# Byte addresses of matmul operands, and attention scores on 128 rows instead of 64, in a two-block fp32 network

## The chip, the cores and the metric

One Trainium2 chip, one of its cores. The metric is the device time of one execution in microseconds, from three runs; one further execution was profiled.

## The reference, cut to what matters

Two transformer blocks over 512 tokens of width 1024, all in float32. The tokens lie along the free axis, the width along partitions (eight tiles of 128).

```
first_block:  16 meta tokens in front, so 528 columns
  h = h + 0.5*swiglu(rmsnorm(h))                       # d_ff 2816
  q,k,v,u,g_attn,g_ssm = rmsnorm(h) @ w_in
  attn = sliding_window_attention(q,k,v)               # 16 query heads, 4 key heads, head size 64
  ssm  = s5 state space model of u, then a gated linear unit
  h = h + (sigmoid(g_attn)*attn + sigmoid(g_ssm)*ssm) @ w_out
  h = h + 0.5*swiglu(rmsnorm(h))                       # meta tokens no longer needed: 512 columns
second_block: 2 layers of  mixer (MLA, then GLA), layer_norm, conv_ffn (d_ff 2816), layer_norm, gated embedding
```

In the attention, a query block of 128 tokens meets the 16 meta keys and the keys of its own and the preceding block: 272 columns, 144 for the first block. A score has a contraction of 64, the head size.

## The kernel before, in words

**How a product is made.** Every large product is done in three passes with operands split in two parts (type fp32r): weights into `whi` and `wlo`, activations into `zh` and `zl` (or `mh`/`ml`, `yh`/`yl`, `gh`/`gl`, `oqh`/`oql`, `ovh`/`ovl`, `pth`/`ptl`). `mm3` (L166) runs for each of the k tiles: `whi` x high part, `whi` x low part, `wlo` x high part, all accumulated in one PSUM bank. The weights are stationary (128 columns), the activations move: 512 columns, or 264 twice in the parts of block 1 that carry the meta tokens (`C528`, tile `mm`). `nat` (L181) has the roles exchanged: the activations are stationary and 256 columns of weights move. Scores, the transposes and a few others are plain f32 matmuls, which the trace shows as two instructions ("passes") each.

**Order.** The program is unrolled. A planner that simulates the program orders the instructions and places the waits; `hold` and `behind` fix the order at a few places. Weights are fetched from HBM with SP's queue into `raw`, split on ScalarE (L84, `whi`) and VectorE (L64, `wlo`), five deep.

**Where the operands lie.** Tiles are placed one after another in a partition, each rounded up to 32 bytes, pools on top of one another in the order in which they are opened. Only the remainder of a start address by 512 matters below, so it is given in brackets. At address 0 lies a scratch of 16384 bytes, then 128 bytes of constants, then pool `cp` (vec 1888 bytes, eight tiles h of 2112, ident 512, and so on) up to 38112. Pool `wp` follows: two tiles `raw`, five `whi` and five `wlo` of 4096 bytes, so that every one of them starts at [224]; a column block of 128 weights is 512 bytes, so every stationary block of `mm3` starts at [224] as well. Pool `sm` ends at 88224, [160]. There pool `zp` begins, which lives as long as the program:

- its tiles have 528 columns in block 1, 2112 bytes = 4 x 512 + 64, and a tag keeps that size for the second block. So `zh0` is at [160], `zl0` at [224], `zh1` at [288], and so on in steps of 64.
- after its 16 operand tiles come `acc`, two `sq` and `R`, and it ends at [416].

Everything opened later starts from [416]. Tiles of 2048 bytes keep that remainder: `yh`/`yl`/`gh`/`gl` in pool `m3`, `kh`, `ovh`, and `pth`, `mh` in `conv_ffn`, are at [416]; `oqh`/`oql` at [448], because the 16 bytes of `rkv` take 32. In the second swiglu the tiles `pi` and `pc` of `tp` have 2064 bytes and take 2080, so that `mh` and `ml` of `f2` begin at [480]. In the first swiglu `mh`/`ml` have 2112 bytes and go through all remainders in steps of 64. In block 1, queries and gates use the columns 16 to 528 of `zh`, which start 64 bytes later.

**The attention.** Two heads' keys lie on partitions 0 to 63 and 64 to 127 of `kw[pp]`, the queries in the same way, and a score reads one half of the partitions:

```
kk = kw[pp][r, max(n - 1, 0), :W]          # r = 64 rows of head s_
last["sc"] = PE.matmul(pq[s_][:, :W], qf[pp * 4 + i][r, n * P:(n + 1) * P], kk)
```

VectorE reads each score bank (L721) with mask and maximum; ScalarE takes the exponentials; PE transposes (L746, L756) and multiplies with the values (L768, L772). Into this stage the loop over `units` sets the state space quarters (L537 to L602), the queries and some of the gate projections.

Of the kernel before, what the change touches and what calls it, by code (L numbers as in the profile page):

```python
# [18 lines left out]
P = 128  # L19
# [34 lines left out]
def body(nc, tc, A, out, es):  # L54
    cp = es.enter_context(tc.tile_pool(name="cp", bufs=1))
    wp = es.enter_context(tc.tile_pool(name="wp", bufs=2))
    sm = es.enter_context(tc.tile_pool(name="sm", bufs=2))
    zp = es.enter_context(tc.tile_pool(name="zp", bufs=1))
    psp = {}
    dr = es.enter_context(tc.tile_pool(name="dr", bufs=1, space=DRAM))  # L60
    V, SC, GP, PE = nc.vector, nc.scalar, nc.gpsimd, nc.tensor
# [44 lines left out]
        psp["tags"] = tags  # L106

    woff = {}


    vec = cp.tile([P, VEC.n], F32, name="vec")
# [104 lines left out]
        return y  # L216

    def split_scaled(src, g, k, n):
        zh = zp.tile([P, n], F32R, name=f"zh{k}")
        zl = zp.tile([P, n], F32R, name=f"zl{k}")  # L220
        act(zh, src, AF.Copy, scale=g)
        stt(zl, src, g, zh.bitcast(F32), ALU.mult, ALU.subtract)
        return zh, zl

    def sumsq(tiles):
        acc = zp.tile([P, T1], F32, name="acc")
        n = tiles[0].shape[1]
        for k, t in enumerate(tiles):
            if k == 0:
                act(acc[:, :n], t, AF.Square)  # L230
            else:
                sq = zp.tile([P, T1], F32, name="sq", bufs=2)
                act(sq[:, :n], t, AF.Square)
                add(acc[:, :n], acc[:, :n], sq[:, :n], None if k == len(tiles) - 1 else GP)
        return acc[:, :n]
# [28 lines left out]

    def token_rsqrt(acc, scale, eps, R=None):

        pst = token_sums(acc)
        r = rsqrt(pst, pst.shape[1], scale, eps)
        if R is None:
            R = zp.tile([P, T1], F32, name="R")[:, :acc.shape[1]]  # L270
        spread_rsqrt(r, R)
        return r, R

# [350 lines left out]
    behind(lambda: mm3(early[2], w, P, 0, z, C528, ks=range(4)))  # L624
    r = rsqrt(pst, 5, 1.0 / D, 1e-6)
    hold["dve"] = last["rsqrt"]
    R = zp.tile([P, T1], F32, name="R")
    hold["act"] = behind(lambda: spread_rsqrt(r, R))
    behind(lambda: mm3(early[2], w, P, 0, z, C528, ks=range(4, 8)))
    with tc.tile_pool(name="sp", bufs=1) as sp, tc.tile_pool(name="f1", bufs=2) as ph:  # L630
# [17 lines left out]
    with tc.tile_pool(name="m1", bufs=1) as mp:  # L648
        att = mp.tile([P, 8, S], F32, name="att")
        with tc.tile_pool(name="m2", bufs=1) as ap_:  # L650
            for i4 in range(4):
                p = proj(wload("w_in", 1024), P, 0, z, C528)
                uf = ap_.tile([P, 4, MC], F32, name="uf", tag="sc", bufs=3)
                for i in range(2):
                    mul(uf[:, :, i * 66:(i + 1) * 66], p[:, i, :264].rearrange("p (m j) -> p j m", j=4),
                        R[:, i * 264:(i + 1) * 264].rearrange("p (m j) -> p j m", j=4))
                nc.sync.dma_start(u_d[i4 * P:(i4 + 1) * P], uf.rearrange("p j m -> p (j m)"))
            kw = []
            for mo in range(2):
                p = proj(wload("w_in", 1024), P, 0, z, C528)  # L660
                f = ap_.tile([P, T1], F32, name="kf", tag=f"sq{mo}")
                mul(v2(f), p[:, :, :264], v2(R))
                g = ap_.tile([P, 3, 272], F32, name=f"kw{mo}")
                GP.tensor_copy(g[:, 0], f[:, :272])
                for n in range(1, 3):
                    GP.tensor_copy(g[:, n, 0:NM], f[:, 0:NM])
                    GP.tensor_copy(g[:, n, NM:], f[:, NM + n * P:NM + (n + 2) * P])
                kw.append(g)
            banks(b=2, q=3, t=2, o=1)
            w = [wload("w_in", 1024), wload("w_in", 1024)]  # L670
            vm = ap_.tile([64, 2, P], F32, name="vm")
# [34 lines left out]
            def scores1(u):  # L706
                pp, n = u
                W = 144 if n == 0 else 272
                mk = mask[:, 272:] if n == 0 else mask[:, :272]
                mt = ap_.tile([P, 4, 64], F32, name="mt", bufs=1)  # L710
                GP.memset(mt, 0.0)
                sc = [ap_.tile([P, 4, 272], F32, name="sc", bufs=3) for _ in range(2)]
                st = [[sm.tile([P, 4], F32, name=f"at{j}{s_}", bufs=2) for j in range(3)] for s_ in range(2)]
                for i in range(4):
                    pq = [pss("q"), pss("q")]
                    for s_ in range(2):
                        r = slice(64 * s_, 64 * s_ + 64)
                        kk = kw[pp][r, max(n - 1, 0), :W]
                        last["sc"] = PE.matmul(pq[s_][:, :W], qf[pp * 4 + i][r, n * P:(n + 1) * P], kk)  # L719
                    for s_ in range(2):  # L720
                        V.tensor_tensor_reduce(sc[s_][:, i, :W], pq[s_][:, :W], mk, 1.0, -3.0e38,  # L721
                                               ALU.add, ALU.max, st[s_][0][:, i:i + 1])
                for s_ in range(2):
                    mx, dn, nb = st[s_]
                    t = sc[s_]
                    kv = 2 * pp + s_
                    sk = sink[:, kv * 4:kv * 4 + 4]
                    tt(mx, mx, sk, ALU.max)
                    ts(nb, mx, -1.0)
                    sub(mx, sk, mx)  # L730
                    act(mx, mx, AF.Exp)
                    for i in range(4):
                        act(t[:, i, :W], t[:, i, :W], AF.Exp, bias=nb[:, i:i + 1], accum_out=dn[:, i:i + 1])
                    add(dn, dn, mx)
                    V.reciprocal(dn, dn)
                    mul(mt[:, :, 32 * s_:32 * s_ + NM], t[:, :, :NM], dn.unsqueeze(2).to_broadcast([P, 4, NM]))
                    mul(t[:, :, NM:W], t[:, :, NM:W], dn.unsqueeze(2).to_broadcast([P, 4, W - NM]), GP if s_ else None)
                live[u] = sc, mt
# [38 lines left out]
            for ui in range(len(units) + 1):  # L777
# [4 lines left out]
                if ui < 4:  # L782
                    query()
                elif 5 <= ui < 8:
                    gate(zp.tile([P, T1], F32, name="acc" if ui == 5 else "sq", bufs=1 if ui == 5 else 2)[:, :S])
                elif ui == 8:
                    with tc.issue_after(last["sc"].ins):
                        for i in range(2):
# [3 lines left out]
                    values1(units[ui - 1])  # L792
        banks(b=6, s=2)
        with tc.tile_pool(name="m3", bufs=2) as gp_:
            yo = []
            for q in range(4):
                yr = gp_.tile([P, 4, P], F32, name="yr")
# [69 lines left out]
    class Norm:  # L867


        def __init__(self, pool, xs, a):  # L870
            self.p, self.xs, self.a = pool, xs, a
            self.aq = zp.tile([P, T1], F32, name="acc")[:, :S]
            self.ad = pool.tile([P, S], F32, name="ad", bufs=1)

        def centre(self):

            pc = pss("s")
            PE.matmul(pc, oness, self.xs[0])
            self.c = zp.tile([P, T1], F32, name="R")[:, :S]
            act(self.c, pc, AF.Copy)  # L880

        def put(self, k, m):
# [192 lines left out]
    with tc.tile_pool(name="a2", bufs=2) as mp:  # L1075
# [36 lines left out]
        Rq = mp.tile([P, S], F32, name="oqR", bufs=1)  # L1112
        okv = operand(ckv, "mla_kv_norm", "ov")
        r, _ = token_rsqrt(sumsq(ckv), 1.0 / 256, 1e-5, Rkv)
        rkv = mp.tile([P, 4], F32, name="ovr", bufs=1)
        V.tensor_copy(rkv, r)
        oq = operand(cq, "mla_q_norm", "oq")
        acc = sumsq(cq)
# [324 lines left out]

    conv_ffn(1, hr, RT2, mixer)
    dump(hr, S)
    psp["cm"].__exit__(None, None, None)


# [96 lines left out]


# [9 lines left out]
```

## Time and profile before

| what | value |
|---|---|
| median of 3 runs | 2670.66 us (2668.88 to 2673.24) |
| the profiled execution | 2667.79 us |
| its span, first to last instruction | 2666.0 us |
| mean granted TensorE clock | 0.991 |
| TensorE busy (matmuls) | 2620.0 us, 13918 matmuls |
| VectorE, ScalarE, GpSimd busy | 1590.7, 959.7, 227.7 us |
| HBM traffic | 229.11 MB read, 11.93 MB written, 90 GB/s |

A matmul's duration in the profile runs from its issue to its modelled end and overlaps the following one, so the busy time is the union of these, and the time from one start to the next is what a matmul costs in a dense chain.

### The profile page before, as it was taken

The numbers are of one execution on the slowest core, as the hardware profiler recorded it, in microseconds if no ns is written. First come the engines' busy times: TensorE is split into PE (matmuls) and PEld (weight loads), VectorE is DVE, ScalarE is ACT, GpSimd is POOL, SyncE is SP. The second block draws the span as 40 slices with busy tenths as digits, with TensorE's granted clock in tenths as the row PEclk, the third lists the DMA queues.
The fourth block names the chain that finished last, engine by engine and source line by source line (L and its number), as shares of the span: only waits on it lengthen the run. The fifth ranks groups of instructions, "written<-read, shape, count | busy, mean of one in ns | idle before, by whom it ended". The sixth has DMA issues, their size and how long they took to land.

```text
span 2666.0 us, 35024 instructions
## 1 busy us (share of the span) xinstructions
PE 2620.0 (98%) x13918; PEld 2186.8 (82%) x13918; DVE 1590.7 (60%) x2794; ACT 959.7 (36%) x1483; POOL 227.7 (9%) x186
## 2 busy tenths in 40 slices
PE   8999999899999999999999999999999999999999
PEld 8999999655888888887888878888778777888887
DVE  7985444685556544468766775555663356655556
ACT  4222223243333222234544454333353234433333
POOL 1000001231000000010000110000200011100020
PEclk9999999999999999999999999999999999999999
DMA  5443233331333333322112223333232221433331
GB/s 176 128 131 112 88 95 122 100 91 52 102 95 92 97 99 96 95 91 68 52 56 60 71 79 103 95 95 95 79 98 61 75 72 58 124 95 95 95 90 68
DMA packets 87748, 243.31 MB, mean 91 GB/s; under 512 B 20081, under 2 KB 26097, under 8 KB 87458
## 3 DMA queue, kind: packets, MB, share of 16 engines
q1 hardware_dynamic: 87586, 241.08, 29.3%
q8 instruction: 110, 1.80, 0.3%
q14 instruction: 52, 0.43, 0.0%
HBM read 229.11 MB, written 11.93 MB: 90 GB/s over the span
## 4 chain that ended last, share of the span: by engine, by line
PE 94%; DVE 3%; issue 1%; ACT 1%; DMA 0%; POOL 0%; SPq 0%; DVEq 0%; POOLq 0%; ACTq 0%
PE ps_b L173 63%; PE mm L173 16%; PE ps_b L189 6%; PE ps_o L1228 1%; PE ps_q L1200 1%; PE ps_o L1365 1%; PE ps_t L1216 1%; PE ps_o L772 1%; PE ps_u L1354 1%; PE ps_q L719 1%; PE ps_t L756 0%; DVE h L64 0%; DVE sq L64 0%; DVE wlo L64 0%; PE ps_q L1198 0%
## 5 line engine op out<-in xcount | busy, mean ns | idle before, releaser
L84 ACT ACTIVATE whi<-raw 128x1024 fp32r<-128x1024 f32 (+2 forms) x418 | 432.2, 1036 | 1050.1 <-PE ps_b L173 701.5
L64 DVE TENSOR_TENSOR wlo<-raw,whi 128x1024 fp32r<-128x1024 f32 (+2 forms) x418 | 516.5, 1238 | 341.2 <-ACT whi L84 337.9
L173 PE MATMUL ps_b<-zh,whi 128*128 128x512 f32 (+1 forms) x1656 | 653.1, 395 | 6.5 <-ACT zh L84 2.3
L173 PE MATMUL ps_b<-zh,wlo 128*128 128x512 f32 (+1 forms) x1656 | 654.7, 396 | 0.0
L173 PE MATMUL ps_b<-zl,whi 128*128 128x512 f32 (+1 forms) x1656 | 642.3, 391 | 0.0
L173 PEld LDWEIGHTS ps_b<-zh,whi 128*128 128x128 f32 (+1 forms) x1656 | 310.8, 188 | 82.6 <-issue 4.6
L173 PEld LDWEIGHTS ps_b<-zl,whi 128*128 128x128 f32 (+1 forms) x1656 | 311.3, 188 | 78.3 <-issue 2.6
L173 PEld LDWEIGHTS ps_b<-zh,wlo 128*128 128x128 f32 (+1 forms) x1656 | 310.7, 188 | 69.2
L173 PE MATMUL ps_b<-mh,wlo 128*128 128x512 f32 x528 | 208.5, 395 | 0.0
L173 PE MATMUL ps_b<-ml,whi 128*128 128x512 f32 x528 | 207.7, 393 | 0.0
L173 PE MATMUL ps_b<-mh,whi 128*128 128x512 f32 x528 | 207.6, 393 | 0.0
L173 PE MATMUL mm<-zh,whi 128*128 128x264 f32 x800 | 165.1, 288 | 6.2 <-ACT whi L84 5.8
L173 PE MATMUL mm<-zl,whi 128*128 128x264 f32 x800 | 164.2, 287 | 0.8 <-DVE zl L81 0.8
L173 PE MATMUL mm<-zh,wlo 128*128 128x264 f32 x800 | 164.1, 287 | 0.6 <-DVE wlo L64 0.6
L81 DVE SCALAR_TENSOR_TENSOR cv<-ps_b,vec,cv 128x511 f32<-128x511 f32 (+1 forms) x176 | 130.4, 745 | 16.0 <-ACT cv L84 14.5
L64 DVE TENSOR_TENSOR h<-h,ps_b 128x512 f32<-128x512 f32 x109 | 74.7, 686 | 104.6 <-PE ps_b L173 100.9
L173 PEld LDWEIGHTS mm<-zh,whi 128*128 128x128 f32 x800 | 126.1, 191 | 6.6 <-ACT whi L84 5.8
L173 PEld LDWEIGHTS mm<-zl,whi 128*128 128x128 f32 x800 | 125.2, 191 | 1.5 <-DVE zl L81 1.5
L173 PEld LDWEIGHTS mm<-zh,wlo 128*128 128x128 f32 x800 | 125.6, 190 | 0.8 <-DVE wlo L64 0.8
L64 POOL TENSOR_TENSOR acc<-acc,sq 128x512 f32<-128x512 f32 (+1 forms) x26 | 38.7, 1489 | 948.3 <-ACT sq L84 909.6
L173 PEld LDWEIGHTS ps_b<-mh,whi 128*128 128x128 f32 x528 | 99.2, 188 | 23.2 <-issue 0.5
L173 PEld LDWEIGHTS ps_b<-mh,wlo 128*128 128x128 f32 x528 | 99.2, 188 | 23.1 <-issue 0.5
(421 smaller groups left out, 4001.0 us busy)
## 6 DMA issues: line engine op xcount, KB each, us to landing
raw<-in_ffn_w_dram SPq DMA_DIRECT2D x130, 512.0 KB, 3.5
raw<-in_w_up_dram SPq DMA_DIRECT2D x88, 512.0 KB, 3.6
raw<-in_w_down_dram SPq DMA_DIRECT2D x44, 512.0 KB, 3.6
raw<-in_w_in_dram SPq DMA_DIRECT2D x32, 512.0 KB, 3.5
raw<-in_mla_o_dram SPq DMA_DIRECT2D x16, 512.0 KB, 3.6
raw<-in_ple_g_dram SPq DMA_DIRECT2D x16, 512.0 KB, 3.6
raw<-in_glu_dram SPq DMA_DIRECT2D x8, 512.0 KB, 3.5
raw<-in_w_out_dram SPq DMA_DIRECT2D x8, 512.0 KB, 3.5
```

What stands on the lines that cost most here:

```text
L64: return (e or V).tensor_tensor(o, a, b, op=op)
L81: return V.scalar_tensor_tensor(o, a, s, b, op0=op0, op1=op1)
L84: return SC.activation(o, a, f, **kw)
L173: last["pe"] = PE.matmul(o[:, i, :c1 - c0], lhs, x[k][r][:, c0:c1], start=(k == 0 and j == 0), stop=(k == kt - 1 and j == 2))
L189: PE.matmul(o[:m, :n], x[k][a][:, t0:t0 + m], w[b][:, kk_ * c + m0:kk_ * c + m0 + n], start=(k == 0 and i == 0), stop=(k == kt - 1 and i = ...
L719: last["sc"] = PE.matmul(pq[s_][:, :W], qf[pp * 4 + i][r, n * P:(n + 1) * P], kk)
L772: PE.matmul(po[64 * s_:64 * s_ + 64], vb[n - 1 + j][:, kv * 64:kv * 64 + 64], pT[s_][:, j], start=False, stop=(j == 1))
L1200: PE.matmul(p[:, :N], d["q"][e][:, bs], d["k"][e][:, :N], start=False, stop=True)
L1216: PE.transpose(pt[:, kt * P:(kt + 1) * P], sc[:, kt * P:(kt + 1) * P], ident)
L1228: PE.matmul(po[:, b * P:(b + 1) * P], vt[:, kt, e * P:(e + 1) * P], pT[:, kt * P:(kt + 1) * P], start=(kt == 0), stop=(kt == b))
L1354: PE.matmul(pu[c][:, :256], ek[b][rows, hc], vt[hh][rows, b])
L1365: PE.matmul(po[hh][-1][64 * c:64 * c + 64, (b % 2) * 256:(b % 2) * 256 + 256], qt[hh][:, n * 64:(n + 1) * 64], s_)
```

## The change

Four things.

1. **Block 1's operands.** A gap of 256 bytes is put at the head of `zp`, and its operand rows get 2560 bytes (5 x 512): `zh0` ... `zl7` then all start at [416], their second halves of 264 columns at [448], and the columns from 16 on at [480]. A gap of 320 bytes in `m3` puts `yh`, `yl`, `gh`, `gl` at [480].
2. **A second operand pool.** After block 1's mixer `zp` is closed and `zq` opened at the same place, with a gap of 320 bytes and tiles of 512 columns (2048 bytes): [160] + 320 = [480], for all its tiles, and it ends at [480]. A gap of 448 bytes in `tp` restores [480] for `f2`, and `rkv` gets a full 512 bytes, so `oqh`, `ovh`, `pth`, `mh`, and `zh4` to `zl7` of GLA lie at [480] too.
3. **The scores.** For each pair of heads there are two key tiles of 128 partitions, one with the first head's keys in the upper half and zeros below, one the other way round. The scores read all 128 partitions of both operands. Four memsets on GpSimd write the zeros, the copies are halved in partitions, and those of the second head go to ScalarE.
4. **The scratch** at address 0 shrinks from 16384 to 2048 bytes, which pays for the room. All addresses fall by 14336 = 28 x 512, no remainder changes by it.

```diff
-    zp = es.enter_context(tc.tile_pool(name="zp", bufs=1))
+    zpc = tc.tile_pool(name="zp", bufs=1)
+    zp = zpc.__enter__()
+    zp.tile([P, 64], F32, name="gap")
...
+    zw, aw = 640, T1
...
     def split_scaled(src, g, k, n):
-        zh = zp.tile([P, n], F32R, name=f"zh{k}")
-        zl = zp.tile([P, n], F32R, name=f"zl{k}")
+        zh = zp.tile([P, zw], F32R, name=f"zh{k}")[:, :n]
+        zl = zp.tile([P, zw], F32R, name=f"zl{k}")[:, :n]
...
+            kz = [[ap_.tile([P, 3, 272], F32, name=f"kw{mo}{e}") for e in range(2)] for mo in range(2)]
+            for gs in kz:
+                for e, g in enumerate(gs):
+                    GP.memset(g[64 - 64 * e:128 - 64 * e], 0.0)
...
-                g = ap_.tile([P, 3, 272], F32, name=f"kw{mo}")
-                GP.tensor_copy(g[:, 0], f[:, :272])
-                for n in range(1, 3):
-                    GP.tensor_copy(g[:, n, 0:NM], f[:, 0:NM])
-                    GP.tensor_copy(g[:, n, NM:], f[:, NM + n * P:NM + (n + 2) * P])
-                kw.append(g)
+                gs = kz[mo]
+                for e, g in enumerate(gs):
+                    r_ = slice(64 * e, 64 * e + 64)
+                    cpy = (lambda o, i: act(o, i, AF.Copy)) if e else GP.tensor_copy
+                    cpy(g[r_, 0], f[r_, :272])
+                    GP.tensor_copy(g[r_, 1:, 0:NM], f[r_, 0:NM].unsqueeze(1).to_broadcast([64, 2, NM]))
+                    for n in range(1, 3):
+                        cpy(g[r_, n, NM:], f[r_, NM + n * P:NM + (n + 2) * P])
+                kw.append(gs)
...
-                        r = slice(64 * s_, 64 * s_ + 64)
-                        kk = kw[pp][r, max(n - 1, 0), :W]
-                        last["sc"] = PE.matmul(pq[s_][:, :W], qf[pp * 4 + i][r, n * P:(n + 1) * P], kk)
+                        last["sc"] = PE.matmul(pq[s_][:, :W], qf[pp * 4 + i][:, n * P:(n + 1) * P],
+                                               kw[pp][s_][:, max(n - 1, 0), :W])
...
         with tc.tile_pool(name="m3", bufs=2) as gp_:
+            gp_.tile([P, 80], F32, name="gap", bufs=1)
...
+    zpc.__exit__(None, None, None)
+    zpc = tc.tile_pool(name="zq", bufs=1)
+    zp = zpc.__enter__()
+    zw, aw = S, S
+    zp.tile([P, 80], F32, name="gap")
...
     with tc.tile_pool(name="rt", bufs=1) as tp, tc.tile_pool(name="f2", bufs=2) as ph:
+        tp.tile([P, 112], F32, name="gap")
...
-        rkv = mp.tile([P, 4], F32, name="ovr", bufs=1)
+        rkv = mp.tile([P, P], F32, name="ovr", bufs=1)[:, :4]
...
-    nc = bacc.Bacc("TRN2", target_bir_lowering=False, num_devices=1)
+    nc = bacc.Bacc("TRN2", target_bir_lowering=False, num_devices=1, dynamic_dma_scratch_size=2048)
```

`acc`, `sq` and `R` are cut to `aw` columns in the same way (528 in block 1, then 512).

## Rows read from the trace of the kernel before

**Rows 1.** Windows by stage: PE, PEld, DVE, ACT, POOL busy (instructions), clock, DMA.
```profile
30.00:418.00 388.00, 388.00 (x3181) 386.58 (x3181) 256.91 (x543) 115.74 (x140) 10.20 (x8) 1.00 0.37 116
486.00:660.00 174.00, 156.44 (x724) 100.18 (x722) 126.91 (x333) 67.53 (x198) 47.53 (x38) 0.94 0.26 76
```

**Rows 2.** Timeline of PE, second swiglu then conv_ffn: start, duration in us.
```profile
1003.07 0.39 PE L173 MATMUL ps_b<-ml,whi 128*128 128x512 f32 x1
1003.75 0.39 PE L173 MATMUL ps_b<-ml,whi 128*128 128x512 f32 x1
...
1810.16 0.39 PE L173 MATMUL ps_b<-ml,whi 128*128 128x512 f32 x1
1810.86 0.40 PE L173 MATMUL ps_b<-ml,whi 128*128 128x512 f32 x1
```

**Rows 3.** Groups by line, second swiglu, 1000.2 to 1021.7: busy us, mean ns.
```profile
L173 PE MATMUL ps_b<-mh,wlo 128*128 128x512 f32 x32 | 12.5, 389 | 0.0
```

**Rows 4.** The same groups in conv_ffn, 1675.1 to 1697.2.
```profile
L173 PE MATMUL ps_b<-ml,whi 128*128 128x512 f32 x32 | 12.7, 395 | 0.0
```

**Rows 5.** Groups of conv_ffn's up projections, 1697.5 to 1741.6, then the second swiglu's, 956 to 999.9.
```profile
L173 PE MATMUL ps_b<-zh,wlo 128*128 128x512 f32 x64 | 25.5, 398 | 0.0
L173 PE MATMUL ps_b<-zl,whi 128*128 128x512 f32 x64 | 25.1, 392 | 0.0
L173 PE MATMUL ps_b<-zh,whi 128*128 128x512 f32 x64 | 25.0, 390 | 0.0
...
L173 PE MATMUL ps_b<-zh,wlo 128*128 128x512 f32 x64 | 25.3, 396 | 0.0
L173 PE MATMUL ps_b<-zh,whi 128*128 128x512 f32 x64 | 25.2, 393 | 0.0
L173 PE MATMUL ps_b<-zl,whi 128*128 128x512 f32 x64 | 24.8, 388 | 0.0
```

**Rows 6.** Groups by line and shape over the whole span.
```profile
L173 PE MATMUL ps_b<-zh,wlo 128*128 128x512 f32 x1632 | 647.0, 397 | 0.0
L173 PE MATMUL ps_b<-mh,wlo 128*128 128x512 f32 x528 | 208.5, 395 | 0.0
L173 PE MATMUL mm<-zh,wlo 128*128 128x264 f32 x800 | 164.1, 287 | 0.6 <-DVE wlo L64 0.6
L189 PE MATMUL ps_b<-wlo,zh 128*128 128x256 f32 x352 | 100.6, 286 | 0.0
L189 PE MATMUL ps_b<-wlo,ovh 128*128 128x256 f32 x64 | 17.9, 280 | 0.0
L1200 PE MATMUL ps_q<-kn,qn 128*128 128x512 f32 x32 | 16.3, 591 | 0.0
L719 PE MATMUL ps_q<-kw,q 64*128 64x272 f32 x96 | 25.1, 438 | 0.5 <-DVE at L721 0.3
L719 PE MATMUL ps_q<-kw,q 64*128 64x144 f32 x32 | 4.3, 325 | 0.0
```

**Rows 7.** Timeline of PE in the first swiglu: pairs of 264 columns.
```profile
100.01 0.40 PE L173 MATMUL mm<-zl,whi 128*128 128x264 f32 x2
100.24 0.41 PE L173 MATMUL mm<-zh,wlo 128*128 128x264 f32 x2
100.49 0.41 PE L173 MATMUL mm<-zh,whi 128*128 128x264 f32 x2
100.74 0.41 PE L173 MATMUL mm<-zl,whi 128*128 128x264 f32 x2
```

**Rows 8.** Timeline of PE around two groups of scores.
```profile
621.89 0.40 PE L173 MATMUL ps_b<-zh,wlo 128*128 128x512 f32 x1
622.21 0.73 PE L719 MATMUL ps_q<-kw,q 64*128 64x272 f32 x4
622.87 1.07 PE L772 MATMUL ps_o<-pT,vb 128*64 128x512 f32 x2
623.88 0.72 PE L719 MATMUL ps_q<-kw,q 64*128 64x272 f32 x2
```

More of the change, by code (lines that the diff above doesn't have):

```diff
@@ L225, in sumsq @@
     def sumsq(tiles):
-        acc = zp.tile([P, T1], F32, name="acc")
+        acc = zp.tile([P, aw], F32, name="acc")
         n = tiles[0].shape[1]
@@ L231, in sumsq @@
             else:
-                sq = zp.tile([P, T1], F32, name="sq", bufs=2)
+                sq = zp.tile([P, aw], F32, name="sq", bufs=2)
                 act(sq[:, :n], t, AF.Square)
@@ L269, in token_rsqrt @@
         if R is None:
-            R = zp.tile([P, T1], F32, name="R")[:, :acc.shape[1]]
+            R = zp.tile([P, aw], F32, name="R")[:, :acc.shape[1]]
         spread_rsqrt(r, R)
@@ L626, in body @@
     hold["dve"] = last["rsqrt"]
-    R = zp.tile([P, T1], F32, name="R")
+    R = zp.tile([P, aw], F32, name="R")
     hold["act"] = behind(lambda: spread_rsqrt(r, R))
@@ L784, in body @@
                 elif 5 <= ui < 8:
-                    gate(zp.tile([P, T1], F32, name="acc" if ui == 5 else "sq", bufs=1 if ui == 5 else 2)[:, :S])
+                    gate(zp.tile([P, aw], F32, name="acc" if ui == 5 else "sq", bufs=1 if ui == 5 else 2)[:, :S])
                 elif ui == 8:
@@ L871, in __init__ @@
             self.p, self.xs, self.a = pool, xs, a
-            self.aq = zp.tile([P, T1], F32, name="acc")[:, :S]
+            self.aq = zp.tile([P, aw], F32, name="acc")[:, :S]
             self.ad = pool.tile([P, S], F32, name="ad", bufs=1)
@@ L878, in centre @@
             PE.matmul(pc, oness, self.xs[0])
-            self.c = zp.tile([P, T1], F32, name="R")[:, :S]
+            self.c = zp.tile([P, aw], F32, name="R")[:, :S]
             act(self.c, pc, AF.Copy)
@@ L1445, in body @@
     dump(hr, S)
+    zpc.__exit__(None, None, None)
     psp["cm"].__exit__(None, None, None)
```

## Prediction

> **What bounds the kernel now.** I read the busy table and the windows by stage first. TensorE has work for 2620 of 2666 us, and in the dense stages for all of it: 388.00 of 388.00 us in the first swiglu [rows 1]. So outside the attention there is no wait to remove, and a change counts there only by what one matmul costs from start to start. The one stage with room is the attention, 486 to 660: PE busy 156.4 of 174 us, VectorE 126.9, clock 0.94 [rows 1].
>
> Next the timeline of dense chains. Three steps of the second swiglu's down projection take 1003.75 - 1003.07 = 0.68 us, 0.227 each; three of conv_ffn's take 1810.86 - 1810.16 = 0.70, 0.233 each [rows 2]. Both are 512 columns of type fp32r with 128 stationary columns at the full clock, both back to back. What differs in the program is where the moving tile starts: [480] in the first, [416] in the second, with the weights at [224] in both. The groups by line say the same with more samples: 389 ns mean against 395 [rows 3, 4]. A duration is the step plus some 162 ns of overlap (389 - 227), so differences of these means can be read as differences of steps. The up projections, whose tiles go through all remainders in steps of 64, lie between: (398 + 392 + 390) / 3 = 393.3 in conv_ffn, (396 + 393 + 388) / 3 = 392.3 in the second swiglu [rows 5]. So the trace has one address class that is quick, and the change puts nearly every 512-column operand into it.
>
> **The change part by part.**
>
> **A, 512-column chains moved to [480].** Each price is the mean now less 389 [rows 3].
> - `zh`/`zl`: 3 x 1632 = 4896 matmuls [rows 6]. Of them 44 projections x 24 = 1056 are the second swiglu's, at 3.3 ns: 3.5 us. The other 3840 at 4.3 ns [rows 5]: 16.5 us. Block 1's queries and gates are among these; they start 64 bytes behind [416], so at [480] too.
> - `mh`/`ml`: 3 x 528 = 1584 [rows 6], of which the second swiglu's 22 x 8 x 3 = 528 are at [480] already. 1056 x 6.3 (395.3 - 389, the middle of that stretch) [rows 3, 4]: 6.7 us.
> - `yh`, `yl`, `gh`, `gl`: 2 x 8 x 12 and 8 x 24 by the code, 384 at [416]; by the rows of [416] in conv_ffn [rows 4], x 6 = 2.3 us.
> - `oq`, `ov`, `pt`: 3 x (96 + 32 + 32) = 480 by the code, at [448] and [416]; by the same rows, x 6 = 2.9 us.
>
> Sum 31.9 us off. These chains hang on nothing else: VectorE and ScalarE, which split the weights, are far from full in the dense stages (256.9 and 115.7 us of 388) [rows 1], and the chains get only 2 to 3% quicker. The bounds: nothing (the address is not the cause, or the price is not carried over), and 36 us (6 ns for each of 6000).
>
> **B, 264-column chains of block 1.** 3 x 800 = 2400 matmuls with `z` [rows 6], 1200 pairs, go from all remainders to [416] and [448] alone. In 388 us there are 3181 matmuls, 0.122 each or 0.244 a pair [rows 1]. Single pairs take 0.23 (100.24 - 100.01) to 0.25 (100.49 to 100.74) [rows 7]; the second of these is `zh6`, which lies at [416] and [448] before as well, though its neighbours do not. A chain of such pairs alone is nowhere in the trace. I take 0, with bounds of -17 us (1200 x 0.014) and +7 (1200 x 0.006). The first swiglu's 1056 `mh` keep rows of 2112 bytes and all remainders: 0.
>
> **C, products with the roles exchanged.** In `nat` the stationary operand moves from a mixture to [480] against moving weights at [224]. 1056 matmuls with `z` at 286 ns, 192 with `ov` at 280, where the stationary one is at [416] [rows 6]. No row has this pairing alone; 0, with 4 us either way (the 6 ns between the rows x 700).
>
> **D, the scores.** Now they are 96 passes of 272 columns on half the array, and 32 of 144 (two block-0 units x 4 x 2 heads x 2 passes): 25.1 and 4.3 us busy, 29.4 together [rows 6]. A pass on all 128 rows costs (591 - 162) / 512 = 0.84 ns a column [rows 6], so 0.228 us for 272 and 0.121 for 144: 96 x 0.228 + 32 x 0.121 = 25.8 us, 3.6 less. Two heads no longer run at once, but the group of four passes took 622.87 - 622.21 = 0.66 us, hardly better than the lone pair that follows 623.88 with its 0.72 [rows 8]; four full passes will take 0.91 and two 0.46. So a group of four loses 0.25 and a lone pair gains 0.2 or more. On top, entering a group costs: the last `zh` pass before one lasts 622.21 - 621.89 = 0.32 instead of 0.23 [rows 8]; at some 32 groups that is 3 us, of which I count 2, since some neighbours (L772) use a part of the array themselves. That makes 5.6 us of PE time. But this stage has 17.6 us without PE work (174 - 156.4) [rows 1] and VectorE is 73% busy in it, so I let half of it turn into longer waits: -3. Bounds: -12 (all of it, and a steadier clock) and +10 (the planner orders this stage anew, and the waits grow by half).
>
> The Trainium skill speaks against this part: its page "TensorEngine Tiling (Array Packing)", section "When to Use Tiling", advises two row tiles for a contraction of 64 or less, worth up to 2x by its table. By that the old scores would be worth 12.9 us busy (half of 25.8) and the change would add 12.9. The same page's "Key Properties" say that a change of tiling mode drains the engine, and the 0.32 against 0.23 agrees. The trace's own sum of 29.4 decides here.
>
> **E, preparing the keys.** Four memsets, key copies by halves, three of each key tile's on ScalarE. GpSimd is busy 10.2 of 388 us before [rows 1] and between the key projections and the first score lie the values (five `nat` products) and four queries; ScalarE's six copies of 256 and 272 columns fit under these. I cost it at 0. Uncovered it would be some 3 us.
>
> **F, closing `zp`, opening `zq`; the scratch.** The first `z` of the second swiglu must wait for the last reader of the bytes under it, the last gate projection, which lies a whole w_out and half of the gated unit earlier. 0. If the planner waits for the whole stage instead, the eight operands are split only after it: some 8 us, a microsecond each for VectorE. The scratch is touched by no instruction of the program; 0.
>
> Sum, with B, C, E and F at 0: -31.9 - 3 = **-34.9 us**. On the profiled execution's own 2667.79 (2666.0 of span and 1.8 around it) that is 2632.9; the median of the runs shown is 2.9 higher, so on that scale 2670.7 - 34.9 = **2636 us**.
>
> **The rivals.**
>
> 1. *Forecast*, -24 to -44 us (2627 to 2647). For it: the quick class is seen in over 500 matmuls of the same kind, with the same weights at the same [224].
> 2. *More*: block 1's pairs turn out cheap (-14) and the attention gives all that PE saves (-5 more): 2617. For it, the 0.23 pair; against it, that its tile is not at [416].
> 3. *Less*: block 1's pairs cost 0.25 (+7) and the planner makes the attention longer by 10: 2653. The attention is the one place where an order can hurt, since VectorE's chain is nearly closed there.
> 4. *The address does nothing by itself*: the 389 belongs to the second swiglu for another reason, such as which pool or bank it works with. Then only D is left: 2668, no difference to be seen. Against it: up and down projections of that stage alternate, with the same weights and banks, and only the tiles at [480] have 389 in all three passes [rows 3, 5]. A sentence in the Trainium skill would have it so: "TensorE: Matmul & The Clock Gate", "Step-by-step: what each phase is for", says that loading the next weights takes no read bandwidth from the running matmul, since each has its own port, which leaves no room for addresses; the 389 against 395 disagrees.
> 5. *Slower*: one remainder for all is the bad case and mixing the good one. For it: the chains at a single remainder in conv_ffn are the slowest (395.3), the mixed ones 2 ns quicker [rows 4, 5]. If [480] is quick only in the second swiglu, everything goes to 395.3: 3840 x 2 + 1056 x 3 + 528 x 6.3 = 14.2 us more, less 3 for D: 2682. It decides from a mean of about 393.5 in the chains after the change on.
>
> **How the numbers follow.** Chances: 1 has 0.74, 2 0.08, 3 0.10, 4 0.03, 5 0.05. The likeliest is 1, so 2636. The range must leave out no more than 2 in 10: 2618 to 2652 holds 1 and about half of 2 and of 3. About 0.2%, 5.3 us, is what a measurement of this kernel can tell from no change. Faster by more: 1, 2, 3 = 0.92; within: 4 = 0.03; slower: 5 = 0.05.
>
> **What would show it.** Right: in the profile after, L173 groups `zh`, `zl`, `mh`, `oqh` of 512 columns at 389 in all three passes, steps of 0.227 in the timeline of both conv_ffn and of the second swiglu; each conv_ffn some 9 us shorter; L719 as 128*128 with passes of about 390 ns, and the passes before them at 0.23. `mm` groups at 285 to 287. Wrong: means over 393 in conv_ffn (4 or 5), 264-column means that leave 283 to 290 (B), waits of PE on VectorE between the scores and L746 that grow by 10 us or clock below 0.94 there (3), an idle PE at about 810 (F).

## The result, and the profile after

The changed kernel takes 2634.5 us (median of 4 runs, 2633.7 to 2639.9), the kernel before 2671.4 beside it (4 runs, 2668.9 to 2673.2): a ratio of 0.9867, 95% interval 0.985 to 0.9884. The forecast was 2636. The profiled execution has 2634.66 us, a span of 2632.8 and a mean clock of 0.993. The span is 33.2 us shorter than before.

Line numbers move: `mm3` is now L176, `nat` L192, the scores L728, the transposes and value products of the attention L756, L766, L778 and L782.

Windows by stage, after; the columns are those of [rows 1]. In order: first swiglu, attention, second swiglu, first `conv_ffn`, GLA.

```profile
28.97:408.00 379.03, 379.03 (x3143) 377.62 (x3143) 254.40 (x539) 115.15 (x140) 8.42 (x6) 1.00 0.38 114
481.80:654.60 172.80, 153.90 (x722) 105.92 (x720) 126.93 (x333) 67.98 (x198) 47.63 (x38) 0.96 0.26 76
819.00:1179.50 360.50, 360.50 (x1600) 298.62 (x1598) 202.34 (x266) 107.18 (x129) 7.94 (x6) 1.00 0.32 96
1500.00:1908.60 408.60, 404.49 (x1780) 333.46 (x1778) 246.29 (x316) 156.76 (x202) 61.99 (x44) 0.99 0.31 92
1908.60:2171.00 262.40, 259.06 (x1530) 208.88 (x1530) 126.82 (x241) 99.29 (x151) 14.52 (x19) 0.99 0.24 74
```

The same instructions took 383.6, 174.15, 364.2, 415.0 and 262.7 us before. The dense stages are shorter by 4.6, 3.7 and 6.4 us, with PE full in the first two as it was. The attention is shorter by 1.3, at a granted clock of 0.96 where it had 0.94; GLA by 0.3. (Windows cut between the same instructions are the ones to compare; a count may differ by a few records that a trace lacks.)

Timeline of PE, after: second swiglu, then the second `conv_ffn` (start, duration in us).

```profile
1000.25 0.39 PE L176 MATMUL ps_b<-mh,whi 128*128 128x512 f32 x1
...
1000.93 0.39 PE L176 MATMUL ps_b<-mh,whi 128*128 128x512 f32 x1
...
2400.11 0.39 PE L176 MATMUL ps_b<-ml,whi 128*128 128x512 f32 x1
...
2400.79 0.39 PE L176 MATMUL ps_b<-ml,whi 128*128 128x512 f32 x1
```

Three steps are 0.68 us in both stages now; [rows 2] had 0.68 and 0.70.

Groups by line and shape over the whole span, after; they answer to [rows 6].

```profile
L176 PE MATMUL ps_b<-zh,wlo 128*128 128x512 f32 x1632 | 635.3, 390 | 0.0
...
L176 PE MATMUL ps_b<-mh,wlo 128*128 128x512 f32 x528 | 206.2, 391 | 0.0
...
L176 PE MATMUL mm<-zh,wlo 128*128 128x264 f32 x800 | 161.9, 284 | 0.0
...
L192 PE MATMUL ps_b<-wlo,zh 128*128 128x256 f32 x352 | 101.9, 290 | 0.0
...
L176 PE MATMUL ps_b<-oqh,whi 128*128 128x512 f32 x96 | 40.4, 422 | 4.6 <-DVE q L66 4.6
...
L728 PE MATMUL ps_q<-kw,q 128*128 128x272 f32 x96 | 28.3, 411 | 0.1
...
L192 PE MATMUL ps_b<-wlo,ovh 128*128 128x256 f32 x64 | 18.1, 283 | 0.0
...
L728 PE MATMUL ps_q<-kw,q 128*128 128x144 f32 x32 | 5.3, 292 | 0.0
```

The 512-column `z` and `mh` went from 397 and 395 to 390 and 391; the 264-column `z` from 287 to 284; `nat` rose from 286 to 290 (with `ov` from 280 to 283). The scores' busy time went from 25.1 + 4.3 to 28.3 + 5.3: up, where I had counted a saving.

### The profile page after: what moved, and what is told of

Its sections match the earlier page's. It is cut to its first block, busy times and chain, and to the rows that moved or that the text cites. A ratio compares the mean times of both kernels' runs of the same rounds, so it can differ in the third digit from the quotient of the medians.

```text
span 2632.8 us, 35040 instructions
## 1 busy us (share of the span) xinstructions
PE 2584.5 (98%) x13918; PEld 2189.5 (83%) x13918; DVE 1590.1 (60%) x2794; ACT 961.4 (37%) x1489; POOL 231.0 (9%) x190
## 4 chain that ended last, share of the span: by engine, by line
PE 93%; DVE 4%; issue 1%; ACT 1%; POOL 0%; DMA 0%; SPq 0%; DVEq 0%; POOLq 0%; ACTq 0%
PE ps_b L176 62%; PE mm L176 15%; PE ps_b L192 6%; PE ps_o L1247 1%; PE ps_q L1219 1%; PE ps_o L1384 1%; PE ps_t L1235 1%; PE ps_o L782 1%; DVE wlo L66 1%; PE ps_u L1373 1%; PE ps_q L728 1%; DVE h L66 0%; DVE sq L66 0%; PE ps_t L766 0%; PE ps_q L1217 0%
## 5 line engine op out<-in xcount | busy, mean ns | idle before, releaser
L176 PE MATMUL ps_b<-zh,whi 128*128 128x512 f32 (+1 forms) x1656 | 649.1, 393 | 8.5 <-DVE acc L66 3.3
L176 PE MATMUL ps_b<-zh,wlo 128*128 128x512 f32 (+1 forms) x1656 | 642.9, 389 | 0.0
L176 PE MATMUL ps_b<-zl,whi 128*128 128x512 f32 (+1 forms) x1656 | 638.4, 389 | 0.0
L176 PEld LDWEIGHTS ps_b<-zh,whi 128*128 128x128 f32 (+1 forms) x1656 | 310.7, 188 | 79.8 <-ACT zh L86 4.1
L176 PEld LDWEIGHTS ps_b<-zl,whi 128*128 128x128 f32 (+1 forms) x1656 | 310.7, 188 | 67.1 <-issue 1.8
L176 PEld LDWEIGHTS ps_b<-zh,wlo 128*128 128x128 f32 (+1 forms) x1656 | 310.5, 188 | 65.3 <-issue 0.8
L176 PE MATMUL ps_b<-mh,wlo 128*128 128x512 f32 x528 | 206.2, 391 | 0.0
L176 PE MATMUL ps_b<-ml,whi 128*128 128x512 f32 x528 | 205.4, 389 | 0.0
L176 PE MATMUL ps_b<-mh,whi 128*128 128x512 f32 x528 | 205.4, 389 | 0.0
L176 PE MATMUL mm<-zh,whi 128*128 128x264 f32 x800 | 162.6, 284 | 5.8 <-ACT whi L86 5.8
L176 PE MATMUL mm<-zl,whi 128*128 128x264 f32 x800 | 162.7, 284 | 3.0 <-DVE zl L83 3.0
L176 PE MATMUL mm<-zh,wlo 128*128 128x264 f32 x800 | 161.9, 284 | 0.0
L176 PEld LDWEIGHTS mm<-zh,whi 128*128 128x128 f32 x800 | 124.4, 189 | 5.8 <-ACT whi L86 5.8
L176 PEld LDWEIGHTS mm<-zl,whi 128*128 128x128 f32 x800 | 124.5, 189 | 3.5 <-DVE zl L83 3.5
L176 PEld LDWEIGHTS mm<-zh,wlo 128*128 128x128 f32 x800 | 124.3, 189 | 0.0
L176 PEld LDWEIGHTS ps_b<-mh,whi 128*128 128x128 f32 x528 | 99.1, 188 | 21.1 <-issue 0.5
L176 PEld LDWEIGHTS ps_b<-mh,wlo 128*128 128x128 f32 x528 | 99.1, 188 | 20.9 <-issue 0.5
```

The source lines that it names most:

```text
L176: last["pe"] = PE.matmul(o[:, i, :c1 - c0], lhs, x[k][r][:, c0:c1], start=(k == 0 and j == 0), stop=(k == kt - 1 and j == 2))
```

## The experiments

In all of them the question is what sets the step of a dense chain, and what each part of the change is worth. *Distance* below means the start of the moving operand less that of the stationary one, modulo 256: `z` at [480] and weights at [224] are at distance 0. The first theory was that [480] itself is the good place of the moving tile; its rival, that only the distance counts.

### 1 and 2. Each half of the change alone

`addr_only` is the kernel after with the keys and scores of the kernel before. `scores_only` is the kernel before with the new keys, the new scores and the scratch of 2048 bytes.

```diff
 # scores_only, on the kernel before
...
-    kk = kw[pp][r, max(n - 1, 0), :W]
-    last["sc"] = PE.matmul(pq[s_][:, :W], qf[pp * 4 + i][r, n * P:(n + 1) * P], kk)
+    last["sc"] = PE.matmul(pq[s_][:, :W], qf[pp * 4 + i][:, n * P:(n + 1) * P],
+                           kw[pp][s_][:, max(n - 1, 0), :W])
...
```

Expected of `addr_only`:

> The changed kernel with the scores as they were before, on 64 rows of the array; all addresses of the 512- and 264-column operands as in the change. Theory 1 (the gain is the addresses): in the profile after, the attention stage gave back 1.3 us of the 33.2 us, so this version stands within 3 us of the changed kernel, 32 to 37 us below the kernel before; attention stage 172 to 175 us, conv_ffn chains at 226.7 ns a step. Theory 2 (the scores on 128 rows gave a real part, 3 us or more, hidden in the stage): 5 us or more above the changed kernel.

Expected of `scores_only`:

> The kernel before with the scores on 128 rows and nothing else but the smaller scratch that makes room for the second pair of key tiles. Theory 1: within 3 us of the kernel before, a ratio of 0.999 to 1.001; chains of 512 columns at the old 231 to 233 ns a step. Theory 2: 4 us or more below, ratio under 0.9985.

Measured: `addr_only` 2640.9 us (2632.1 to 2643.6), ratio 0.989, interval 0.9872 to 0.9909. `scores_only` 2667.5 (2663.2 to 2671.2), ratio 0.9995, interval 0.9986 to 1.0004. A group of dense passes in `scores_only`, and then the attention's window in it:

```profile
L173 PE MATMUL ps_b<-mh,wlo 128*128 128x512 f32 x528 | 208.5, 395 | 0.0
```

```profile
486.40:660.60 174.20, 155.05 (x729) 105.72 (x728) 127.12 (x333) 67.96 (x198) 47.44 (x38) 0.97 0.27 77
```

The stage takes 174.2 us with the new scores and 174.15 without them, but at granted clocks of 0.97 and 0.94 [rows 1], so equal times here do not mean equal work; the dense groups stay where they were. The interval of `scores_only` allows 3.7 us less and 1.1 us more, so it does not exclude a saving of 3. The median of `addr_only` is 6.4 us above that of the kernel after, which is theory 2 by its words, and 2.8 above that of `after_again` (experiment 10). These differences go with the granted clock of each execution: at 0.993 `addr_only` took 2632.1 us and the kernel after 2633.7 to 2634.7, at 0.990 2639.1 and 2639.9; `scores_only` took 2670.3 at 0.991 where the kernel before took 2667.2 to 2670.7, and 2666.6 to 2667.7 at 0.992 where it took 2668.7. So at equal clocks the addresses give the gain, and the scores nothing that can be told from none.

### 3. Everything moved by 32 bytes

```diff
+    cp.tile([P, 8], F32, name="pad")
     vec = cp.tile([P, VEC.n], F32, name="vec")
```

Weights now start at [256], operands at [0]; all distances are unchanged.

Expected:

> The changed kernel with 32 unused bytes at the very start of its first pool, so that weights go from [224] to [256] and the operands from [480] to [0]: every remainder moves, every distance stays. Theory D (the distance between the start of the moving tile and the start of the stationary block decides): nothing changes, 389 ns mean and 2632 to 2638 us. Theory A (the moving tile's own remainder decides, and [480] is the good one): the 512-column groups go to 393 to 395 ns, 7300 matmuls x 4 to 6 ns, 2664 to 2678 us.

Measured: 2640.4 us (2637.1 to 2643.1), ratio 0.9886, interval 0.9872 to 0.9901.

```profile
L177 PE MATMUL ps_b<-zh,wlo 128*128 128x512 f32 x1632 | 636.4, 391 | 0.0
...
L177 PE MATMUL ps_b<-mh,wlo 128*128 128x512 f32 x528 | 206.2, 391 | 0.0
```

The total is 2 us above the range of theory D and 24 below that of theory A; the gain stays. [480] is nothing special; the theory that I started from falls.

### 4. The weights alone moved by 64 bytes

```diff
+    wp.tile([P, 16], F32, name="pad", bufs=1)
...
-    zp.tile([P, 64], F32, name="gap")
+    zp.tile([P, 48], F32, name="gap")
...
-    zp.tile([P, 80], F32, name="gap")
+    zp.tile([P, 64], F32, name="gap")
```

Weights at [288]; the operands stay at [480], so distance 192.

Expected:

> The changed kernel with the weights alone moved by 64 bytes, [224] to [288]; the gaps of the operand pools are cut by 64 bytes, so that the moving operands stay at [480]. Theory D: the distance is now 192, that of [416] against [224] in the kernel before, whose chains ran at 395 ns mean, 233 ns a step; 7300 matmuls x 6.5 ns = 47 us slower than the change, 2675 to 2688 us. Theory A: no difference, 389 ns, 2632 to 2638 us.

Measured: 2684.6 us (2681.1 to 2685.8), ratio 1.005, interval 1.0034 to 1.0067: slower than the kernel before.

```profile
L177 PE MATMUL ps_b<-zh,wlo 128*128 128x512 f32 x1632 | 644.5, 396 | 0.0
...
L177 PE MATMUL ps_b<-mh,wlo 128*128 128x512 f32 x528 | 209.1, 396 | 0.0
...
L177 PE MATMUL mm<-zh,wlo 128*128 128x264 f32 x800 | 165.8, 289 | 0.6 <-DVE wlo L67 0.6
...
L193 PE MATMUL ps_b<-wlo,zh 128*128 128x256 f32 x352 | 100.1, 285 | 0.0
```

All operands are where the change puts them, and 64 bytes at the weights cost 44 us against `shift_all32` measured beside it (50 against the kernel after as first measured); 47 were expected. One group goes the other way: `nat`, whose distance is now 64, is back at 285 from the 290 of the kernel after.

### 5. Distance 0 instead of 256

```diff
-    zp.tile([P, 80], F32, name="gap")
+    zp.tile([P, 16], F32, name="gap")
```

In the pool `zq`; the second block's operands lie at [224], as the weights do.

Expected:

> The changed kernel with the second pool's gap at 64 bytes, so that all operands from the second swiglu on start at [224] and not [480], weights at [224]: the distance is 0 and not 256. Theory D with a period of 256: 389 ns and 2632 to 2638 us. Theory A, or a distance with a period of 512: the 512-column groups of these stages at 393 to 395 ns, some 6300 matmuls x 4 to 6 ns, 2660 to 2672 us.

Measured: 2639.7 us (2638.0 to 2643.5), ratio 0.9886, interval 0.9871 to 0.9901, with `mh` at 389 to 391 as after. The total is again some 2 us above what was expected of it. Moving by 256 bytes changes no step; modulo 256 is enough.

### 6 and 7. Other distances, one for each stage

`sweep1` and `sweep2` change only the gaps, so that each stage of one kernel works at a distance of its own while its up projections stay at 0.

```diff
 # sweep1 (sweep2)
-    zp.tile([P, 64], F32, name="gap")
+    zp.tile([P, 80], F32, name="gap")                          # (96)
...
-            gp_.tile([P, 80], F32, name="gap", bufs=1)
+            gp_.tile([P, 56], F32, name="gap", bufs=1)         # (24)
...
-        tp.tile([P, 112], F32, name="gap")
+        tp.tile([P, 80], F32, name="gap")                      # (72)
...
         with tc.tile_pool(name=f"cf{li}", bufs=2) as ph:
+            ph.tile([P, (80, 8)[li]], F32, name="gap", bufs=1) # ((56, 112))
```

Expected of `sweep1`:

> The kernel after, with five distances between the moving start and the stationary start (always [224]) instead of one: yh/yl/gh/gl at [448] (distance 224, modulo 256), mh/ml of the second swiglu at [352] (128), mh/ml/pth/ptl of the first conv_ffn at [288] (64), of the second at [0] (32), block 1's zh/zl at [480] and [0] (0 and 32), queries and gates at [32] (64). All other operands stay at distance 0. Theory (the distance sets the step of a dense chain): 0 stays at 226.7 ns; 224 has 233, as in the kernel before where runs of distance 224 alone had 232.8; 32, 64 and 128 lie between, 227 to 230, as the mixed pairs of the kernel before had 227.2 (128 then 64) and 229.1 (64 then 128). Rival (only distance 0 is quick and the quick mixed pairs are alternations): all four others at 233. Other rival (some distance is better than 0): a chain below 226. Block 1's 264-column z, 120.0 at distances 192/224 and 122.9 at 128/160: 119 if a short distance is good for them too, 123 if the rival holds. Total by the theory some 2635 to 2645, by the first rival about 2650.

Expected of `sweep2`:

> As the other sweep, with yh/yl/gh/gl at [384] (distance 160), mh/ml of the second swiglu at [320] (96), mh/ml/pth/ptl of the first conv_ffn at [192] (224), of the second at [416] (192, which repeats the kernel before), block 1's zh/zl at [32] and [64] (64 and 96), queries and gates at [96] (128). Theory: 192 gives 233.2 again, in a kernel where everything around it runs at 226.7; 224 and 160 about 233; 96 between 227 and 230. Rival (only 0 is quick): 96 at 233 too. 264-column z 120 to 122 by the theory. Total 2645 to 2650 by either.

Measured: one execution each, 2647.2 and 2659.4 us, beside 2672.2 for the kernel before. The step is read from the timeline as (last start - first start) / (count - 1). First and last `mh` pass of a chain of 96 in the kernel after, then in `sweep1` for three stages, then in `sweep2` at the distance of the kernel before:

```profile
922.73 0.39 PE L176 MATMUL ps_b<-mh,whi 128*128 128x512 f32 x1
944.26 0.39 PE L176 MATMUL ps_b<-mh,wlo 128*128 128x512 f32 x1
...
931.44 0.40 PE L176 MATMUL ps_b<-mh,whi 128*128 128x512 f32 x1
953.60 0.39 PE L176 MATMUL ps_b<-mh,wlo 128*128 128x512 f32 x1
...
1669.59 0.40 PE L176 MATMUL ps_b<-mh,whi 128*128 128x512 f32 x1
1691.35 0.39 PE L176 MATMUL ps_b<-mh,wlo 128*128 128x512 f32 x1
...
2344.10 0.40 PE L176 MATMUL ps_b<-mh,whi 128*128 128x512 f32 x1
2366.27 0.40 PE L176 MATMUL ps_b<-mh,wlo 128*128 128x512 f32 x1
...
2356.30 0.40 PE L176 MATMUL ps_b<-mh,whi 128*128 128x512 f32 x1
2378.47 0.40 PE L176 MATMUL ps_b<-mh,wlo 128*128 128x512 f32 x1
```

| distance | chain | starts, us | count | step, ns |
|---|---|---|---|---|
| 0 | after, `mh`, second swiglu | 922.73 to 944.26 | 96 | 226.6 |
| 32 | sweep1, `mh`, second `conv_ffn` | 2344.10 to 2366.27 | 96 | 233.4 |
| 64 | sweep1, `mh`, first `conv_ffn` | 1669.59 to 1691.35 | 96 | 229.1 |
| 96 | sweep2, `mh`, second swiglu | 938.19 to 960.37 | 96 | 233.5 |
| 128 | sweep1, `mh`, second swiglu | 931.44 to 953.60 | 96 | 233.3 |
| 160 | sweep2, `g`, block 1 | 771.72 to 816.46 | 192 | 234.2 |
| 192 | sweep2, `mh`, second `conv_ffn` | 2356.30 to 2378.47 | 96 | 233.4 |
| 224 | sweep1, `g`, block 1 | 765.19 to 809.75 | 192 | 233.3 |

Of the two ways on record the truth takes most of the rival's: only 0 is quick, 64 is a third of the way, all other multiples of 32 cost 233 to 234. Three distances have a second place in these kernels: 64 has 228.9 ns and 128 has 232.4 in block 1's gates (`sweep1`, `sweep2`), 224 has 233.4 in the first `conv_ffn` of `sweep2`. My "lie between" was wrong for 32, 96 and 128, and so was reading it off mixed pairs. The total of `sweep2`, expected at 2645 to 2650 by either way, is a miss of 9 us: with the steps measured, its chains and the 264-column pairs add some 22 us to the kernel after, where the expectation leaves room for some 15.

### 8. The low weights alone moved by 64 bytes

```diff
         hi = wp.tile([P, 1024], F32R, tag="whi", name="whi", bufs=5)
+        if not last.get("pad"):
+            last["pad"] = wp.tile([P, 16], F32, name="pad", bufs=1)
         lo = wp.tile([P, 1024], F32R, tag="wlo", name="wlo", bufs=5)
...
```

With both `zp` gaps 64 bytes smaller, the operands stay at [480] and `whi` at [224]; `wlo` is at [288]. One pass in three has distance 192.

Expected:

> The kernel after, with the five tiles of wlo alone moved by 64 bytes, from [224] to [288]; whi stays at [224] and the moving operands at [480]. So a pass with whi has distance 0 and a pass with wlo 192. It asks whose distance counts. Theory (the pass's own stationary operand): the step from a wlo pass to the next is 233.3 and the other two of the three stay at 226.7; some 2370 wlo passes of 512 columns x 6.6 give 15.6 us, total about 2650. Rival (the stationary operand that is being loaded for the following pass while this one streams): the pass ahead of the wlo pass, which streams while wlo is loaded, has 233.3, and the wlo pass itself 226.7; the same total. Other rival (only chains at one distance are quick): all three at 230 or more, total 2660.

Measured: 2669.8 us (one execution, beside 2669.5 for the kernel before): the whole gain is gone. Groups of the second swiglu in this kernel; a k tile issues them from the last line to the first:

```profile
L178 PE MATMUL ps_b<-mh,wlo 128*128 128x512 f32 x175 | 69.5, 397 | 0.0
L178 PE MATMUL ps_b<-ml,whi 128*128 128x512 f32 x175 | 68.6, 392 | 0.0
L178 PE MATMUL ps_b<-mh,whi 128*128 128x512 f32 x176 | 68.5, 389 | 0.0
```

From the start of a pass to the next start it is 228.4 (`whi` with the high part), 229.2 (`whi` with the low) and 235.8 ns (`wlo`) (means of some 500 each, `z` and `mh` together, from the trace), 231.1 over all. The pass whose own stationary operand is off pays 9 ns over 226.7, more than the 6.6 of a chain that is off throughout; and the two that are at distance 0 pay 2 each. So none of the three came out whole. The first rival (the operand being loaded for the next pass) is not borne out, since the pass ahead of `wlo` has 229.2 only; the theory names the dear pass, but not that the others pay; and the total is above the 2660 of the last rival, which had all three at 230 or more. A single stranger among three costs two thirds of what three cost (4.4 of 6.6 ns a pass).

### 9 and 10. Block 1 carried to distance 0, and the kernel after once more

`halves_0` is the kernel after with the halves of 264 columns 1280 bytes apart, for `z` and `mh` of the first swiglu; `split_halves` writes the two halves there, and `mh`/`ml` are made in the same way.

```diff
-    z = [split_scaled(t, vcol("ffn1_norm", k), k, T1) for k, t in enumerate(h)]
+    z = [split_halves(t, vcol("ffn1_norm", k), k) for k, t in enumerate(h)]
...
-        swiglu(ph, z, R, C528, T1, "ffn1_w1", "ffn1_w3", "ffn1_w2", h, lambda: next(par, None), early)
+        swiglu(ph, z, R, C584, T1, "ffn1_w1", "ffn1_w3", "ffn1_w2", h, lambda: next(par, None), early)
...
+    C584 = ((0, 264), (320, 584))
...
```

Expected of `halves_0`:

> The kernel after, with block 1 carried on: in the first swiglu the two halves of 264 columns of zh/zl and mh/ml lie 1280 bytes apart, at [480] and [224], so that both start at distance 0 (modulo 256) from the weights; in block 1's mixer the row is moved within its tile so that the columns from 16 on are at distance 0 and the halves at 192 and 224 as in the kernel after. Nothing is computed differently. If distance 0 is the quick one for 264 columns too: steps fall from 120.0 (z) and about 121.6 (mh) to about 118, which a half at distance 0 after one at 32 had; 2112 z and 1056 mh matmuls of the first swiglu give 4 and 4 us, so the stage from the start to the key projections is some 8 us shorter and the ratio to the kernel after 0.997. Rival (a chain of 264 columns depends on its address only through the mixture of two): 120 to 122 as in all other arrangements, time as the kernel after.

Expected of `after_again`:

> The changed kernel once more, unchanged, on the chip of the other run, as its measure: ratio to the kernel before 0.985 to 0.989, about 2637.

Measured: `halves_0` 2640.9 us (2637.2 to 2645.3), ratio 0.9894, interval 0.9877 to 0.991; `after_again` 2638.1 (2631.2 to 2641.1), ratio 0.9874, interval 0.9857 to 0.9891. In `halves_0`:

```profile
L177 PE MATMUL mm<-zh,wlo 128*128 128x264 f32 x800 | 162.9, 285 | 0.0
...
L177 PE MATMUL mm<-mh,wlo 128*128 128x264 f32 x352 | 71.7, 284 | 0.0
```

The gain expected did not come. The steps of `z` in the first swiglu, 1989 of them, have a mean of 120.8 ns at distance 0, where the kernel after, with halves at 192 and 224, has 120.0; those of `mh` went from 121.6 to 121.2. At distance 0 the chains of `z` differ among themselves: 120.0 from 100 to 150 us, 121.3 in another (384 passes, 246.51 to 292.99); why was not followed. The rule of the 512-column chains does not carry over to 264 columns, and no kernel here beats the one after.

The second profile of the same kernel tells what its executions differ by. The attention's window in `after_again`:

```profile
481.90:660.00 178.10, 160.19 (x722) 109.23 (x720) 126.99 (x333) 67.27 (x197) 47.48 (x38) 0.92 0.26 74
```

It has 178.1 us at a granted clock of 0.92, against 172.8 at 0.96 in the first profile: 5.3 of the 6.5 us by which the spans differ (2639.3 and 2632.8). PE is busy 6.3 us longer there and idle 1.0 less, so it is the passes that got longer. Differences of 5 us between these kernels' totals are therefore not read as effects here.

## Why the prediction was right, point by point

**A, 512-column chains: right, in place and in size.** Joining each start with the instruction that the program issues there, the intervals shrank by 21.2 us for `z`, 6.8 for `mh`, 2.5 for `y` and `g`, 1.5 for `oq` and `ov`: 32.0, against 31.9 forecast. `pt` gave 2.1 back. About 1.5 of that is the clock: at the end of the first `conv_ffn`, behind 16 products of one column (1899.4 to 1901.2), the granted clock falls to 0.5 (1.2 GHz), and eight passes of `pt` take 0.39 to 0.43 us from start to start; before, none did at that place.

```profile
1901.73 0.39 PE L176 MATMUL ps_b<-pth,wlo 128*128 128x512 f32 x1
1901.96 0.59 PE L176 MATMUL ps_b<-pth,whi 128*128 128x512 f32 x1
1902.35 0.63 PE L176 MATMUL ps_b<-ptl,whi 128*128 128x512 f32 x1
1902.77 0.63 PE L176 MATMUL ps_b<-pth,wlo 128*128 128x512 f32 x1
```

Another 0.3 is PE's wait for VectorE's `ad` at the start of that `conv_ffn`, 2.8 us after and 2.5 before. The fall is no sure part of the change: at this place nine of the twelve traces have it; at the start of the second `conv_ffn` three have one and at its end seven (there the kernel after does, `after_again` does not). So -30 in all. Each `conv_ffn` was to be some 9 us shorter: the second is, by 8.5 (379.4 to 370.9), the first, with those eight passes, by 6.5 (377.8 to 371.3). The forecast that `oqh` comes to 389 was wrong: 422 for the first pass, from 429. Its median is 393; 23 of its 96 passes last 470 to 770 ns, as many as before, and three of these are at a clock below 1, right behind PE's wait of 4.6 us for `q`. The upper bound of 36 us rested on 6000 passes, where the list above it adds up to 6816, or 41 us; the measured fall is inside either.

The reason given was half right. "One address class is quick" holds, and the class is not a place but a relation of two places [rows 3, 4]: distance 0 has 226.7 ns, 192 (which [416] against [224] is) 233.4. That fits the middling 392 to 393 of the up projections, too [rows 5]. In `conv_ffn` before, `zh` alternates between distances 192 and 64 and `zl` between 0 and 128; the steps of the table, averaged over the three passes, give 230.8 ns, and the trace has 231.1 there. The average is not the whole rule: for `wlo_64`, where the stationary starts differ within a chain, it would give 228.9, and 231.1 were measured.

**Rival 4 falls**: `weights_64` and `wlo_64` take the gain away by 64 bytes at one operand, with pools and banks as they were. "TensorE: Matmul & The Clock Gate" of the Trainium skill, section "Step-by-step: what each phase is for", gives the weight load a port of its own; the two runs, where only the place of the weights differs, show that the pair's addresses count all the same, by 6.6 ns a pass in the first. Which part of the memory the two share was not tried.

**Rival 5, the slower one, names a case that exists** and that its own argument placed wrongly. A single distance for all chains can be the bad case: `weights_64` took 2684.6, where the rival's sum said 2682. It is decided by the distance at the weights, not by uniformity: of the arrangements tried for all of these chains, all at 0 is the quickest, all at 192 the slowest, the mixtures (the kernel before, `wlo_64`) between.

**B, block 1's pairs: forecast 0, measured -4.1 us** (`z` in the first swiglu, 122.3 to 120.0 ns a pass), inside the bounds of -17 and +7. The 0.25 of the one pair that lay at [416] before [rows 7] did not carry over to a chain of such pairs; that its neighbours made it so is not shown.

**C, roles exchanged: forecast 0, measured +2.8 us** (2.4 with `z`, 118.0 to 119.5 ns; 0.4 with `ov`), inside the bound of 4. In `nat` distance 0 is the dearer one: 119.4 ns at 0, 117.3 at 64 (`weights_64`). This is most of why GLA, with some 1.7 us saved in its 512-column chains, is only 0.3 shorter.

**D, the scores: forecast -3, measured -1.3** (`scores_only` 0.9995, which leaves room for -3.7 to +1.1, and is no difference at equal clocks, so 0 in the sum below). The forecast is inside that interval, but the sum it rests on, "25.8 us, 3.6 less, and 2 for the entries", failed. Its 29.4 us were busy time with overlap, and not what a group costs from its start to the next instruction; so was the 0.72 of the pair at 623.88 [rows 8], set beside a 0.66 from start to start. The timeline after, around groups of four and two passes:

```profile
614.31 0.39 PE L176 MATMUL ps_b<-zh,wlo 128*128 128x512 f32 x1
614.54 1.08 PE L728 MATMUL ps_q<-kw,q 128*128 128x272 f32 x4
615.45 0.60 PE L766 MATMUL ps_t<-ident,sc 128*128 128x128 f32 x4
...
616.99 0.72 PE L728 MATMUL ps_q<-kw,q 128*128 128x272 f32 x2
```

The entry is free now, 614.54 - 614.31 = 0.23 against 0.32 [rows 8], as forecast; the four passes take 0.91, as forecast, against 0.66. What I had not counted is how many groups there are of each size. By the traces some 12 lone pairs (13 before, 11 after) gain 0.09 inside (0.65 to 0.56, the median) and most of them about 0.1 at the entry, some -2 us; 6 fours lose 0.255 less 0.1, and 4 sixes (1.11 to 1.47 us) 0.36 less 0.1: +2. The nine other groups, of eight and ten passes or with 144 columns, are not in this sum. Two heads at once on half the array are worth 0.25 us for four passes; only pairs that stand alone pay more for changing the shape than they get. The Trainium skill, in "TensorEngine Tiling (Array Packing)", section "Theoretical Speedup", would have up to 2x for a contraction of 64; here four passes had 0.91 / 0.66 = 1.4, and the changes of shape took it back.

VectorE's chain remains what PE waits for in that stage. Waits of PE there, after (total, times, longest, us):

```profile
PE ps_t L756 <- DVE mt L66: 6.8, 5, 2.6
PE ps_b L592 <- DVE sq L66: 4.0, 2, 3.0
PE ps_b L176 <- DVE acc L66: 3.3, 1, 3.3
```

The first two were 6.6 and 4.5 us before, the third 1.6. PE was without work for 18.1 us of the window before and 18.9 after. Rival 3's mechanism, a longer attention, did not come from the order; an execution at a lower clock makes one of half that size (`after_again`).

**E and F: 0, right.** PE is full on both sides of the first `z` of the second swiglu, at about 819 us, so the new pool holds nothing up (after, columns of [rows 1]; the second swiglu's window is above):

```profile
654.60:819.00 164.40, 164.38 (x730) 136.26 (x731) 84.43 (x109) 59.12 (x77) 10.22 (x6) 1.00 0.33 101
```

From the last key projection to the attention it is 37.0 us (444.8 to 481.8) where it was 37.2.

**The sum.** -30.0 - 4.1 + 2.8 + 0 = -31.3, and the span fell by 33.2. Of the other 1.9 us, 1.2 lie in the 32 products `ps_s<-gc,L` of GLA (4.7 to 3.5 us from each start to the next); the rest was not followed. The granted clock may have a part in this, which is not separated: 0.991 in the profile before, 0.993 after. The mechanism of A was right but for what the class is; that the total came out almost exactly is luck besides, since three terms costed at or near 0 had errors of both signs (-4, +3, +3).

## What to carry to other kernels

In a dense chain of three passes that is PE-bound, look at where the moving and the stationary tile begin, modulo 256 bytes: the same remainder gave 226.7 ns for 512 columns of fp32r, every other one tried but 64 bytes some 233, and one stray operand among three cost most of the gain. Prove it by moving one operand by 64 bytes, and for each shape by itself, since 264 columns and exchanged roles did not follow the rule. For a change of array shape count groups by size, from the start of a group to the start of what follows, and not busy time.

## What the hardware showed that I had not expected

- The rule of 256: a step of 226.7 ns at distance 0, 229.1 at 64, 233 to 234 at 32, 96, 128, 160, 192 and 224 (232.4 for 128 in its second place); the same at distance 256 and with everything moved by 32 bytes.
- It is not local to a pass: with one pass of three at 192, that pass has 235.8 ns and the two at distance 0 have 228.4 and 229.2.
- 264 columns follow no such rule: the steps of `z` in the first swiglu have means of 120.0 ns (halves at 192 and 224), 120.0 (0 and 32), 120.8 (both 0), 122.0 (64 and 96), 122.3 (the mixture before) and 122.9 (128 and 160).
- The granted clock in the attention differs between executions of one kernel, 0.96 and 0.92, and the stage is 5 us longer at the lower one.
